# An RWKV recurrence whose triangular inverses are formed two groups at a time, in a loop pinned to its source order

## The chip, the cores and the metric

The kernel runs on one core of a Trainium2 chip. The metric is the device time of one execution in microseconds (us), from the runs shown below. TensorE (PE) does the matmuls, VectorE (DVE), ScalarE (ACT) and GpSimd (POOL) the elementwise work, and SyncE (SP) issues most DMA transfers. Each engine takes its instructions in the order in which the program lists them.

## What is computed

A trunk of two layers on 1024 tokens of 1024 channels in float32. Layer 0 mixes a gated convolution with differential attention, layer 1 is RWKV-7 time mixing; each is followed by a layer norm, a gated feed-forward network (FFN) and another norm. The change concerns the RWKV recurrence:

```
def wkv7_scan(r, w, k, v, a, b):                 # 16 heads x 64
    def step(S, inp):
        r_t, w_t, k_t, v_t, a_t, b_t = inp
        sa = jnp.einsum('bhvk,bhk->bhv', S, a_t)
        S = S * w_t[:, :, None, :] + sa[..., None] * b_t[:, :, None, :] + v_t[..., None] * k_t[:, :, None, :]
        return S, jnp.einsum('bhvk,bhk->bhv', S, r_t)
    ...

def rwkv7_time_mix(x, ...):
    ...
    o = wkv7_scan(r, decay, k, v, -kk, kk * a)
    mu = jnp.mean(o, -1, keepdims=True)
    var = jnp.mean(jnp.square(o - mu), -1, keepdims=True)
    o = ((o - mu) * lax.rsqrt(var + GN_EPS)) * gn_g + gn_b
    o = o + jnp.sum(r * k * r_k, -1, keepdims=True) * v
    return (o * g) @ w_o, v_first
```

## The kernel before

The program runs mixer 0 (to about 560 us), FFN 1 (to about 1200 us), the RWKV projections R, K and V with their preparation (to about 1655 us), the recurrence loop (to about 2011 us), and then the rest of the output projection and FFN 2.

The recurrence is computed in chunks of 64 tokens, in a form that replaces the token-by-token scan by matmuls and one triangular inverse for each chunk and head (formed in two blocks of 32 and joined). The work is cut into eight **units**: four quarters q of the tokens, two groups g of eight heads. The loop is `for i in range(n_u + 1)`. Each iteration calls `chunks` twice (h = 0 and 1), and each call works on two chunks at once, one of unit i-1 and one of unit i. The chain of one call is fixed by the data:

- S1 (PE, line 1410), copied to `xs` by ACT (1412); products `po` (1416) that wait for nothing else fill PE meanwhile;
- S2 (PE, 1421), copied to `xv` by ACT (1423);
- S3 (PE, 1430); DVE then forms `sm` (1432) and from it the next chunk's `xv` (1438, two for each chunk). S1 of the next call reads that `xv`;
- S4 (PE, 1444), the output, copied to `O` by ACT (1446).

Between these steps `chunks` calls `pump` four times, so p runs from 0 to 7 in an iteration: p0 and p4 lie between S1 and S2, p1 and p5 between S2 and S3, p2 and p6 between S3's DVE work and S4, p3 and p7 after S4. The table `PB` says which side work is issued at each pump, `PE_` which pieces of the output projection ("d") and loads for it ("e"). The side work:

- x, `prepare1` of unit i+3: four groups of matmuls `am` (1277) with a DVE multiply (1289), stores of `tD` and loads of `G`, then the inverse: for r = 1 to 30 a multiply (1310) and an add (1312) on DVE, and stores of the inverse in two layouts, `tT` and `tU` (1321, 1322). One unit has only 64 rows (two blocks of each of eight heads in four chunks), so `G` is loaded twice and the rows j of the inverse are split by parity over the two halves of the partitions.
- y, `prepare2` of unit i+1: loads of `TT` and `xs` from these stores (1354, 1356), two groups of small matmuls `mg` (1367, 1374), the copies `pm` on DVE (1369), and the loads of `xs`, `xv` and `rb` (1382 to 1386).
- z, `prepare3` of unit i+1: `am` products, a POOL multiply and the transposes `bt` (1339); g, the gates.
- t, `finish`, the **tail** of unit i-2, a group norm: on DVE a sum `gmu` (1453), a scale and a subtraction (1456); on ACT a square (1459); on DVE a sum (1461) and a scale (1462); on POOL a power (1463); on DVE a product (1464); then on PE the transposes `yt` (1472) in two groups of four. Its four steps are issued at p3, twice at p4, and at p5.

Products read operands from two tiles `bk` and `z` that are loaded anew for each group of eight matmuls (1268, 1271). In the V-projection stage ahead of the loop the table `VS` issues steps of the chain `pre`, which prepares the first units.

A scheduler sets each engine's order from dependences and priorities. S1 to S3 are marked with `high_priority`; otherwise an instruction may be put on its engine well before or after the place it has in the source. In FFN 1 a region is already under `manual_schedule(engines=ORDERED)`, where PE, DVE and ACT keep the order of the source; the recurrence loop is not.

Of the kernel before, what the change touches and what calls it, by code (L numbers as in the profile page):

```python
# [10 lines left out]
F32 = mybir.dt.float32  # L11
# [5 lines left out]
P = 128  # L17
# [24 lines left out]
PB = {"0": "y1 x1 g1 x1", "1": "g1", "2": "g0 y1 x1", "3": "g1 y1 t1 x1", "4": "x0 y1 x1 g1 t1 t1 g0", "5": "z1 g1 x0 g0 t1", "6": "z1", "7": "g1 x1 z1 g1"}  # L42
# [18 lines left out]
class Kern:  # L61
# [798 lines left out]
    def rwkv(self, xf, then):  # L860
# [419 lines left out]
        def prepare1(q, g, u):  # L1280

            XS = []
            tD = pd.tile([2, 32, 32, 32], F32, name=self.nm("tD"))
            for s in range(2):
                xs = self.U("xs")
                bk, zv = chunk_operands(q, g, s, 0)
                for i in range(2):
                    pv = chunk_products(bk, zv, i)
                    nc.vector.tensor_mul(xs[:, i * 512:i * 512 + 512].rearrange("p (h c t) -> p h c t", h=2, t=64), pv, mbc[0])
                    if i == 1:  # L1290
                        xv = xs.rearrange("p (h t) -> p h t", t=64)
                        for b in range(2):
                            nc.sync.dma_start(tD[b, s * 16:s * 16 + 16].rearrange("h s t -> s h t"), xv[s * 64 + b * 32:s * 64 + b * 32 + 32, :, b * 32:b * 32 + 32])
                    yield
                XS.append(xs)
            u["XS"] = XS
# [4 lines left out]
            yield  # L1301
            R = self.W("R", F32)
            Gv = G.rearrange("p (s t) -> p s t", t=32)
            Rv = R[:, :512].rearrange("p (j t) -> p j t", t=32)
            for pa in range(2):
                nc.vector.tensor_copy(Rv[half(pa)], G[half(pa), :].rearrange("p (j a t) -> p j a t", a=2, t=32)[:, :, pa, :])
            for r in range(1, 31):
                nj, nt = (r + 1) // 2, 31 - r
                tv = R[:, 512:512 + nj * nt].rearrange("p (j t) -> p j t", t=nt)
                nc.vector.tensor_tensor(tv, Rv[:, :nj, r:r + 1].broadcast_to([P, nj, nt]),  # L1310
                                        Gv[:, r:r + 1, r + 1:].broadcast_to([P, nj, nt]), op=ALU.mult)
                nc.vector.tensor_add(Rv[:, :nj, r + 1:], Rv[:, :nj, r + 1:], tv)
                if r in (8, 16):
                    yield
            for pa in range(2):
                nc.vector.memset(R[half(pa), :512][:, pa::34], 1.0)
            nc.vector.tensor_copy(G[:, :512].rearrange("p (t j) -> p t j", j=16), Rv.rearrange("p j t -> p t j"))
            tT = pd.tile([2, 32, 16, 2, 32], F32, name=self.nm("tT"))
            tU = pd.tile([32, 32, 32], F32, name=self.nm("tU"))
            for pa in range(2):  # L1320
                nc.sync.dma_start(tT[:, :, :, pa, :].rearrange("b h j t -> (b h) j t"), Rv[half(pa)])
                nc.sync.dma_start(tU[:, :, pa * 16:pa * 16 + 16], G[pa * 64:pa * 64 + 32, :512].rearrange("p (t j) -> p t j", j=16))
            u["tT"], u["tU"] = tT, tU
            yield
# [21 lines left out]
        def prepare2(q, g, u):  # L1346
# [4 lines left out]
            for s in range(2):  # L1351
                nc.gpsimd.memset(tv[64 * s + 32:64 * s + 64, :, 0:32], 0.0)
                for b in range(2):
                    nc.sync.dma_start(tv[64 * s + 32 * b:64 * s + 32 * b + 32, :, b * 32:b * 32 + 32],
                                      tT[b, s * 16:s * 16 + 16].rearrange("h j a t -> (j a) h t"))
                nc.sync.dma_start(XS[s].rearrange("p (h t) -> p h t", t=64)[s * 64:s * 64 + 32, :, 0:32],
                                  tU[s * 16:s * 16 + 16].rearrange("h t j -> t h j"))
# [10 lines left out]
            for s in range(2):  # L1368
                nc.vector.tensor_copy(pm[hi[s], :].rearrange("p (h j a) -> p h j a", a=2, j=16), pt[hi[s], :512].rearrange("p (h a j) -> p h j a", a=2, j=16))
# [119 lines left out]
        p1, p2, p3 = ((lambda i, f=f: f(*units[i], U_[i]) if i < n_u else none) for f in (prepare1, prepare2, prepare3))  # L1489
# [6 lines left out]
        pre = chain(p1(0), p1(1), p3(0), p2(0), p1(2))  # L1496
# [31 lines left out]
        tail = none  # L1528
        for i in range(n_u + 1):
            g1, g2, g3, tl = p1(i + 3), p2(i + 1), p3(i + 1), tail  # L1530
            count = [0]

            def pump():
                p = count[0]
                count[0] += 1
                for a in PB.get(f"{p}", "").split():
                    drain({"x": g1, "y": g2, "z": g3, "g": gen, "t": tl}[a[0]], int(a[1:]))
# [12 lines left out]
            drain(g1)  # L1550
            tail = finish(*units[i - 1], U_[i - 1]["O"]) if i else none
        for _ in range(5):
# [158 lines left out]
```

## Time and profile before

| | us |
|---|---|
| median of 3 runs | 2770.09 (2766.3 to 2771.7) |
| profiled execution | 2769.9 |
| its span, first to last instruction | 2768.1 |
| PE busy in the span | 2596.0 (94%) |
| DVE busy | 1937.0 (70%) |
| recurrence loop, first copy of S1 to the end of the last unit | 348, of which PE is busy 280.42 and DVE 253.80 |
| the loop's units, in order | 49, 37, 46, 46, 38, 39, 31, 38, 24 |

A unit here is the stretch from the first copy `xs` (line 1412) of one iteration to that of the next. The profile counts an engine as busy while it executes an instruction; PE's time includes matmuls that run at the lower of its two clock levels, 1.2 GHz. PEclk is the granted clock as a share of the full 2.4 GHz.

### The profile page before, as it was taken

How to read it: one execution, taken by the hardware profiler on the slowest of the kernel's cores; microseconds unless marked ns; L12 is line 12 of the kernel's file. 1: busy time of each engine (PE TensorE's matmuls, PEld its weight loads, DVE VectorE, ACT ScalarE, POOL GpSimd, SP SyncE). 2: the span in 40 equal slices, each digit the busy share in tenths (PEclk: the TensorE clock that was granted, in tenths of full speed). 3: DMA queues.
4: the chain of work that ended last, by engine and by line, in shares of the span. 5: the costliest groups of instructions: out<-in, count | busy, mean ns of one | idle time of the engine just before them, and what ended most of it. 6: DMA issues, size and time to landing. Idle time of an engine off the chain costs nothing. (4 is left out here: it accounts for less than half of the span.)

```text
span 2768.1 us, 37639 instructions
## 1 busy us (share of the span) xinstructions
PE 2596.0 (94%) x14736; PEld 2133.1 (77%) x14736; DVE 1937.0 (70%) x3013; ACT 1123.2 (41%) x1706; POOL 275.4 (10%) x247
## 2 busy tenths in 40 slices
PE   8999989989999999999997988688898999999998
PEld 6777778778888888877876766677776888888887
DVE  4655655598888865667778656786758888887673
ACT  3333332344444441426676223333425444444330
POOL 0000000100000003010011011343420000000000
PEclk9999999999999999999998999887999999999999
DMA  5111223212222273633256678786441222225660
GB/s 168 54 46 44 73 88 110 85 61 92 76 84 92 73 264 117 218 128 114 91 183 236 221 219 234 182 195 171 174 147 46 94 82 92 76 84 184 230 217 31
DMA packets 208674, 358.07 MB, mean 129 GB/s; under 512 B 88944, under 2 KB 118256, under 8 KB 208496
## 3 DMA queue, kind: packets, MB, share of 16 engines
q1 hardware_dynamic: 198704, 320.01, 36.5%
q0 software_dynamic: 9792, 35.66, 3.4%
q8 instruction: 116, 1.90, 0.3%
q14 instruction: 62, 0.51, 0.1%
HBM read 255.46 MB, written 95.94 MB: 127 GB/s over the span
## 5 line engine op out<-in xcount | busy, mean ns | idle before, releaser
L137 PE MATMUL up<-x,wu 128*128 128x512 f32 x1232 | 481.8, 393 | 18.5 <-DVE u L312 8.2
L138 PE MATMUL up<-x,wu 128*128 128x512 f32 x1232 | 482.9, 392 | 0.3 <-DVE x L145 0.2
L139 PE MATMUL up<-x,wu 128*128 128x512 f32 x1232 | 482.0, 391 | 0.0
L137 PEld LDWEIGHTS up<-x,wu 128*128 128x128 f32 x1232 | 232.8, 189 | 71.0 <-ACT x L144 14.4
L138 PE MATMUL dn<-wdl,gt 128*128 128x512 f32 x704 | 273.7, 389 | 0.0
L137 PE MATMUL dn<-wdh,gt 128*128 128x512 f32 x704 | 272.2, 389 | 0.3 <-ACT xf L179 0.3
L139 PE MATMUL dn<-wdh,gt 128*128 128x512 f32 x704 | 272.3, 389 | 0.0
L138 PEld LDWEIGHTS up<-x,wu 128*128 128x128 f32 x1232 | 233.1, 189 | 50.7 <-DVE x L145 2.7
L139 PEld LDWEIGHTS up<-x,wu 128*128 128x128 f32 x1232 | 233.0, 189 | 48.7
L254 ACT CAST wu<-ws 128x512 fp32r<-128x512 f32 x176 | 109.3, 623 | 288.4 <-PE up L139 198.8
L137 PE MATMUL pr<-xv,wph 128*128 128x512 f32 x384 | 154.0, 405 | 9.7 <-DVE kp L1156 7.7
L137 PE MATMUL pj<-x,wih 128*128 128x512 f32 x384 | 153.1, 409 | 7.5 <-ACT x L144 7.5
L115 DVE TENSOR_TENSOR wdl<-raw,wdh 128x1024 fp32r<-128x1024 f32 x88 | 109.7, 1246 | 68.7 <-ACT wdh L114 55.5
L138 PE MATMUL pr<-xv,wph 128*128 128x512 f32 x384 | 153.9, 401 | 3.5 <-DVE xv L915 3.5
L139 PE MATMUL pr<-xv,wpl 128*128 128x512 f32 x384 | 154.2, 402 | 2.6 <-DVE wpl L115 2.6
L139 PE MATMUL pj<-x,wil 128*128 128x512 f32 x384 | 153.8, 401 | 0.2 <-DVE wil L115 0.2
L138 PE MATMUL pj<-x,wih 128*128 128x512 f32 x384 | 153.8, 400 | 0.0
L137 PEld LDWEIGHTS dn<-wdh,gt 128*128 128x128 f32 x704 | 132.2, 188 | 27.8 <-ACT xf L179 0.5
L138 PEld LDWEIGHTS dn<-wdl,gt 128*128 128x128 f32 x704 | 132.2, 188 | 27.7 <-DVE wdl L115 0.3
L139 PEld LDWEIGHTS dn<-wdh,gt 128*128 128x128 f32 x704 | 132.2, 188 | 27.3
L114 ACT CAST wdh<-raw 128x1024 fp32r<-128x1024 f32 x88 | 92.6, 1052 | 108.6 <-DMA raw<-wdn 103.5
L254 ACT CAST wu<-wr 128x512 fp32r<-128x512 f32 x132 | 81.4, 623 | 125.1 <-PE up L139 62.8
(319 smaller groups left out, 5230.8 us busy)
## 6 DMA issues: line engine op xcount, KB each, us to landing
wr<-wup SPq DMA_DIRECT2D x88, 512.0 KB, 4.2
raw<-wdn SPq DMA_DIRECT2D x88, 512.0 KB, 4.2
G<-cv POOLq DMA_DIRECT2D x44, 512.0 KB, 2.9
gr<-G SPq DMA_DIRECT2D x88, 256.0 KB, 4.1
bk<-bkS SPq DMA_DIRECT2D x32, 512.0 KB, 5.9
res<-spill SPq DMA_DIRECT2D x24, 512.0 KB, 4.6
raw<-win SPq DMA_DIRECT2D x22, 512.0 KB, 3.7
spill<-res SPq DMA_DIRECT2D x16, 512.0 KB, 2.8
```

Source lines behind the costliest of these rows:

```text
L114: self.nc.scalar.copy(hi, raw)
L115: self.nc.vector.tensor_sub(lo, raw, hi.bitcast(F32))
L137: nc.tensor.matmul(ps, ah, bh, start=first, stop=False, **kw)
L138: nc.tensor.matmul(ps, ah, bl, start=False, stop=False, **kw)
L139: nc.tensor.matmul(ps, al, bh, start=False, stop=last, **kw)
L254: nc.scalar.copy(t[:, lo], src)
```

## The change

1. `prepare1` now treats both groups g of a quarter at once. The 128 partitions hold (g, block, head), so nothing is doubled: 30 multiplies and 30 adds now serve two units, each on r*(31-r) elements in a row (30 to 240) in place of ((r+1)//2)*(31-r). The two parity copies, and the permutation in the `pm` copies, go; the reordering copy of `G` moves from DVE to ACT; `R` is loaded by a DMA of its own; the stores of `tT` and `tU` become whole rows.
2. `prepare1` has 16 steps for each pair: eight products, the loads, six pieces of five r each, and a final one. A table `XB` says in which unit and pump each is issued. All of quarter 0 and 11 of the 16 steps of quarter 1 lie ahead of the loop. Quarter 1's rest is in unit 0; quarter 2 has its products in unit 0, its inverse at p5 to p7 of unit 1 and p0 to p2 of unit 2, and quarter 3 the same two units later.
3. The loop is put under `manual_schedule(engines=ORDERED)`: PE, DVE and ACT keep the order of the source. SP and POOL are still scheduled.

Lines of the new file are two higher up to `prepare1` and two lower from line 1354 on.

```
-PB = {"0": "y1 x1 g1 x1", "1": "g1", "2": "g0 y1 x1", "3": "g1 y1 t1 x1", "4": "x0 y1 x1 g1 t1 t1 g0", "5": "z1 g1 x0 g0 t1", "6": "z1", "7": "g1 x1 z1 g1"}
+PB = {"0": "y1 x g1", "1": "x g1", "2": "y1 x", "3": "g1 y1 t1 x", "4": "y1 x g1 t1 t1", "5": "z1 g1 x t1", "6": "x z1", "7": "g1 x z1 g1"}
+XB = {0: ("1 2", "1 2", "1 2", "1 2", "2", "1 2", "2", "2"), 1: ("2", "", "", "", "", "2", "2", "2"),
+      2: ("2 3", "2 3", "2 3", "3", "2 3", "3", "3", "3"), 3: ("3", "", "", "", "", "3", "3", "3"), 4: ("3", "3", "3", "", "3")}
...
-            G = self.U("G")
-            tDf = tD.rearrange("b h s t -> (b h) (s t)")
-            nc.sync.dma_start(G[0:64, :], tDf)
-            nc.sync.dma_start(G[64:128, :], tDf)
+            G, R, tmp = self.U("G"), self.U("R"), self.H("tv")
+            tDf = tD.rearrange("g b h s t -> (g b h) (s t)")
+            nc.sync.dma_start(G, tDf)
+            nc.sync.dma_start(R, tDf)
...
-            for pa in range(2):
-                nc.vector.tensor_copy(Rv[half(pa)], G[half(pa), :].rearrange("p (j a t) -> p j a t", a=2, t=32)[:, :, pa, :])
             for r in range(1, 31):
-                nj, nt = (r + 1) // 2, 31 - r
-                tv = R[:, 512:512 + nj * nt].rearrange("p (j t) -> p j t", t=nt)
-                nc.vector.tensor_tensor(tv, Rv[:, :nj, r:r + 1].broadcast_to([P, nj, nt]),
-                                        Gv[:, r:r + 1, r + 1:].broadcast_to([P, nj, nt]), op=ALU.mult)
-                nc.vector.tensor_add(Rv[:, :nj, r + 1:], Rv[:, :nj, r + 1:], tv)
-                if r in (8, 16):
+                nt = 31 - r
+                tv = tmp[:, :r * nt].rearrange("p (j t) -> p j t", t=nt)
+                nc.vector.tensor_tensor(tv, Rv[:, :r, r:r + 1].broadcast_to([P, r, nt]),
+                                        Gv[:, r:r + 1, r + 1:].broadcast_to([P, r, nt]), op=ALU.mult)
+                nc.vector.tensor_add(Rv[:, :r, r + 1:], Rv[:, :r, r + 1:], tv)
+                if r % 5 == 0:
                     yield
...
-            nc.vector.tensor_copy(G[:, :512].rearrange("p (t j) -> p t j", j=16), Rv.rearrange("p j t -> p t j"))
+            nc.scalar.copy(G.rearrange("p (t j) -> p t j", j=32), Rv.rearrange("p j t -> p t j"))
...
-            for pa in range(2):
-                nc.sync.dma_start(tT[:, :, :, pa, :].rearrange("b h j t -> (b h) j t"), Rv[half(pa)])
-                nc.sync.dma_start(tU[:, :, pa * 16:pa * 16 + 16], G[pa * 64:pa * 64 + 32, :512].rearrange("p (t j) -> p t j", j=16))
+            nc.sync.dma_start(tT.rearrange("g b h j t -> (g b h) (j t)"), R)
+            for g in range(2):
+                nc.sync.dma_start(tU[g].rearrange("h t j -> h (t j)"), G[g * 64:g * 64 + 32, :])
...
-        pre = chain(p1(0), p1(1), p3(0), p2(0), p1(2))
+        pre = chain(part(p1[0], 9), part(p1[1], 4), part(p1[0], 6), p3(0), p1[0], part(p1[1], 5), p2(0), part(p1[1], 2))
...
+        region = ExitStack()
+        region.enter_context(self.tc.manual_schedule(engines=ORDERED))
         for i in range(n_u + 1):
...
+                    if a == "x":
+                        for j in XB.get(i, ("",) * 8)[p:p + 1]:
+                            for c in j.split():
+                                drain(p1[int(c)], 1)
+                        continue
...
+        region.close()
```

The change moves instructions. Three places follow; a tile's name carries a running number.

PE, iteration 4 of the loop, before: the end of S3 (L1430) of call h = 0 and the start of S1 (L1410) of h = 1, with the tail's first transposes `yt` of unit 2 (L1472) and operands of `prepare3` (L1277, L1339) put among its matmuls.

```order
L1430 MATMUL sq_14568<-xv_14336,bkt_14481 64x64
L1410 MATMUL sq_14796<-xv_13828,xs_12651 64x64
L1416 MATMUL po_14797<-xv_13828,rb_13826 64x64
L1472 MATMUL yt_14857<-ident,O_13562 128x128 x4
L1277 MATMUL am_14890<-z_11379,bk_14886 128x128 x4
L1339 MATMUL bt_14897<-ident,bk_14886 128x128 x4
L1410 MATMUL sq_14796<-xv_13832,xs_12753 64x64
```

PE at the same place after: the end of the `po` products (L1414), then `yt` (now L1470), then S2 (L1419) for both chunks, the operands of `prepare3` (L1279, L1337), the second `yt`, and S3 (L1428).

```order
L1414 MATMUL po_14551<-xv_14140,rb_14138 64x64
L1414 MATMUL po_14551<-xv_14144,rb_14138 64x64
L1470 MATMUL yt_14615<-ident,O_13404 128x128 x4
L1419 MATMUL sq_14550<-xs_14560,TT_13443 64x64 x8
L1419 MATMUL sq_14550<-xs_14570,TT_13947 64x64 x8
L1279 MATMUL am_14648<-z_11379,bk_14644 128x128 x4
L1337 MATMUL bt_14655<-ident,bk_14644 128x128 x4
L1470 MATMUL yt_14661<-ident,O_13404 128x128 x4
L1428 MATMUL sq_14550<-xv_13700,bkt_13764 64x64
```

All four transposes of the first group now stand after S1 and its products and ahead of S2, and S2 and S3 stand behind them.

DVE, iteration 5, before: the tail of unit 3 (L1453, L1454, L1456) among the recurrence's `sm` and `xv` (L1432, L1438) of call h = 0 and an inverse (L1310, L1312).

```order
L1432 TENSOR_TENSOR sm_14918<-sq_14796,ST 128x256
L1310 TENSOR_TENSOR R_14965<-R_14965,G_14843 128x110
L1440 TENSOR_TENSOR ST<-sm_14918,gc 128x256
L1312 TENSOR_TENSOR R_14965<-R_14965 128x5x22
L1453 TENSOR_REDUCE gmu_15257<-O_14066 128x16
L1310 TENSOR_TENSOR R_14965<-R_14965,G_14843 128x105
L1454 TENSOR_SCALAR gmu_15257<-gmu_15257 128x16
L1312 TENSOR_TENSOR R_14965<-R_14965 128x5x21
L1456 TENSOR_TENSOR O_14066<-O_14066,gmu_15257 128x1024
L1432 TENSOR_TENSOR sm_14929<-sq_14796,ST 128x256
L1310 TENSOR_TENSOR R_14965<-R_14965,G_14843 128x120
L1438 TENSOR_TENSOR xv_14332<-sm_14929,gc 64x256
L1438 TENSOR_TENSOR xv_14336<-sm_14929,gc 64x256
```

DVE, iteration 5, after: `sm` and `xv` of call h = 0 (L1430, L1436), the `pm` copies (L1367), then the whole tail of unit 3 (L1451 to L1462).

```order
L1430 TENSOR_TENSOR sm_14849<-sq_14758,ST 128x256
L1436 TENSOR_TENSOR xv_14590<-sm_14849,gc 64x256
L1436 TENSOR_TENSOR xv_14594<-sm_14849,gc 64x256
L1367 COPY pm_14855<-mg_14854 32x512 x2
L1451 TENSOR_REDUCE gmu_14943<-O_13908 128x16
L1452 TENSOR_SCALAR gmu_14943<-gmu_14943 128x16
L1454 TENSOR_TENSOR O_13908<-O_13908,gmu_14943 128x1024
L1459 TENSOR_REDUCE gvr_14996<-Y_14994 128x16
L1460 TENSOR_SCALAR gvr_14996<-gvr_14996 128x16
L1462 TENSOR_TENSOR O_13908<-O_13908,gvr_14996 128x1024
```

The tail's first sum moved from between the two `sm` to behind both chunks' `xv` and the `pm` copies; the inverse is not in this iteration any more.

SP at the loop's start, before: the loads of unit 0's operands `xv` and `rb`, the last store of `vS` but one, and the stores of products `tD`; unit 0's loads of `TT` stand 20 rows further up.

```order
L1384 DMA xv_12425<-vS_8475 64x4x256
L1386 DMA rb_12423<-rS_8479 64x4x256
L1384 DMA xv_12429<-vS_8475 64x4x256
L1244 DMA vS_8476<-vtok_12402 128x8x128
L1386 DMA rb_12423<-rS_8479 64x4x256
L1250 DMA bvS_8474<-bv_12223 128x1024
L1271 DMA z_11379<-aS_8478 64x2x256 x2
L1293 DMA tD_12432<-xs_12433 32x16x32 x2
```

SP at the loop's start, after: the last `vS` store, a `z`, the joint loads of `G` and `R`, unit 0's `TT` (L1352) and then its `xs`, `xv` and `rb` (L1380 to L1384).

```order
L1246 DMA vS_8476<-vtok_12392 128x8x128
L1273 DMA z_11380<-aS_8477 64x2x256
L1302 DMA G_12413<-tD_11787 128x1024
L1303 DMA R_12414<-tD_11787 128x1024
L1252 DMA bvS_8474<-bv_12273 128x1024
L1352 DMA TT_12418<-tT_12298 32x16x32 x4
L1380 DMA xs_11447<-aS_8477 64x4x256
L1382 DMA xv_12500<-vS_8475 64x4x256
L1384 DMA rb_12498<-rS_8479 64x4x256
L1380 DMA xs_11539<-aS_8477 64x4x256
L1382 DMA xv_12504<-vS_8475 64x4x256
```

Unit 0's loads of `TT`, `xs`, `xv` and `rb` moved from ahead of the last `vS` stores to behind the loads of `G` and `R` for quarter 1.

## Rows read from the trace of the kernel before

**Rows 1.** Windows of the loop: length; busy PE, PEld, DVE, ACT, POOL; clock; DMA; GB/s.

```profile
1749.00:1795.00 46.00, 33.81 (x564) 30.45 (x566) 40.23 (x112) 16.65 (x37) 22.10 (x19) 0.87 0.72 177
...
1841.00:1879.00 38.00, 28.79 (x520) 25.45 (x516) 35.97 (x87) 15.25 (x34) 18.27 (x15) 0.89 0.76 186
...
sum 348.00, PE 280.42 PEld 239.51 DVE 253.80 ACT 124.04 POOL 130.22; mean PE 31.16 PEld 26.61 DVE 28.20 ACT 13.78 POOL 14.47
```

**Rows 2.** Groups of DVE instructions in the loop, shapes apart: count, busy, mean ns, idle.

```profile
L1438 DVE TENSOR_TENSOR xv<-sm,gc 64x256 f32<-64x256 f32 x48 | 26.9, 561 | 0.9
...
L1432 DVE TENSOR_TENSOR sm<-sq,ST 128x256 f32<-128x256 f32 x30 | 12.6, 419 | 28.5 <-PE sq L1430 28.5
...
L1369 DVE COPY pm<-mg 32x512 f32<-32x512 f32 x14 | 9.7, 690 | 5.6 <-PE mg L1367 5.4
...
L1310 DVE TENSOR_TENSOR R<-R,G 128x30 f32<-128x30 f32 x12 | 2.2, 187 | 0.2
...
L1310 DVE TENSOR_TENSOR R<-R,G 128x128 f32<-128x128 f32 x6 | 1.7, 290 | 0.2
```

**Rows 3.** Waits of PE in the loop: us in total, times, longest.

```profile
PE sq L1410 <- DVE xv L1438: 24.6, 6, 8.4
...
PE am L1277 <- issue: 12.3, 4, 5.6
...
PE am L1277 <- DMA bk<-bkS: 11.4, 4, 6.0
...
PE yt L1472 <- DVE O L1464: 2.2, 1, 2.2
```

**Rows 4.** Windows, two neighbouring stretches of units 4 to 6.

```profile
1877.40:1894.50 17.10, 16.53 (x290) 14.60 (x288) 14.16 (x43) 3.74 (x10) 3.75 (x2) 0.50 0.72 171
1894.50:1911.60 17.10, 13.94 (x216) 12.18 (x214) 6.76 (x16) 9.91 (x23) 11.64 (x10) 1.00 0.48 99
```

**Rows 5.** Timeline of PE, S1 in these stretches: start us, us, then idle before.

```profile
1877.20 0.33 PE L1410 MATMUL sq<-xv,xs 128*64 128x64 f32 x2 [4.98 <-DVE xv L1438]
...
1878.10 1.11 PE L1410 MATMUL sq<-xv,xs 128*64 128x64 f32 x14
...
1895.29 0.68 PE L1410 MATMUL sq<-xv,xs 128*64 128x64 f32 x14
```

**Rows 6.** Timeline, the tail of unit 7, alone after the loop.

```profile
2011.83 1.22 DVE L1453 TENSOR_REDUCE gmu<-O 128x16 f32<-128x1024 f32 x1 [1.00 <-ACT O L1446]
...
2013.30 1.22 DVE L1456 TENSOR_TENSOR O<-O,gmu 128x1024 f32<-128x1024 f32 x1
...
2014.69 1.06 ACT L1459 ACTIVATE Y<-O 128x1024 f32<-128x1024 f32 x1 [2.89 <-DVE O L1456]
...
2016.30 1.21 DVE L1461 TENSOR_REDUCE gvr<-Y 128x16 f32<-128x1024 f32 x1
...
2018.28 2.92 POOL L1463 TENSOR_TENSOR gvr<-gvr,mhalf 128x16 f32<-128x16 f32 x1 [8.93 <-DVE gvr L1462]
...
2021.74 1.22 DVE L1464 TENSOR_TENSOR O<-O,gvr 128x1024 f32<-128x1024 f32 x1
```

**Rows 7.** Timeline of SP and PE at the loop's start.

```profile
1620.17 2.22 SPq L1354 DMA_DIRECT2D TT<-tT  x4
...
1662.12 1.07 SPq L1293 DMA_DIRECT2D tD<-xs  x2
...
1644.02 0.39 PE L137 MATMUL pr<-xv,wph 128*128 128x512 f32 x1
...
1644.24 0.39 PE L138 MATMUL pr<-xv,wph 128*128 128x512 f32 x1
...
1660.70 0.33 PE L1410 MATMUL sq<-xv,xs 128*64 128x64 f32 x2
```

**Rows 8.** DMA issues from 1500 to 2012 us: count, KB, median us to landing.

```profile
tD<-xs SPq DMA_DIRECT2D x32, 64.0 KB, 3.7
...
xv<-vS SPq DMA_DIRECT2D x16, 256.0 KB, 6.5
```

More of the change, by code (lines that the diff above doesn't have):

```diff
@@ new lines, in prepare1 @@
+        def prepare1(q, us):
+            tD = pd.tile([2, 2, 32, 32, 32], F32, name=self.nm("tD"))
+            for g in range(2):
+                us[g]["XS"] = XS = []
+                for s in range(2):
+                    xs = self.U("xs")
+                    XS.append(xs)
+                    bk, zv = chunk_operands(q, g, s, 0)
+                    for i in range(2):
+                        pv = chunk_products(bk, zv, i)
+                        nc.vector.tensor_mul(xs[:, i * 512:i * 512 + 512].rearrange("p (h c t) -> p h c t", h=2, t=64), pv, mbc[0])
+                        if i == 1:
+                            xv = xs.rearrange("p (h t) -> p h t", t=64)
+                            for b in range(2):
+                                nc.sync.dma_start(tD[g, b, s * 16:s * 16 + 16].rearrange("h s t -> s h t"), xv[s * 64 + b * 32:s * 64 + b * 32 + 32, :, b * 32:b * 32 + 32])
+                        yield
+            G, R, tmp = self.U("G"), self.U("R"), self.H("tv")
+            tDf = tD.rearrange("g b h s t -> (g b h) (s t)")
+            nc.sync.dma_start(G, tDf)
+            nc.sync.dma_start(R, tDf)
+            yield
+            Gv, Rv = (x.rearrange("p (s t) -> p s t", t=32) for x in (G, R))
+            for r in range(1, 31):
+                nt = 31 - r
[4 more added lines that the diff above has]
+                if r % 5 == 0:
+                    yield
+            nc.vector.memset(R[:, ::33], 1.0)
+            nc.scalar.copy(G.rearrange("p (t j) -> p t j", j=32), Rv.rearrange("p j t -> p t j"))
+            tT = pd.tile([2, 2, 32, 32, 32], F32, name=self.nm("tT"))
+            tU = pd.tile([2, 32, 32, 32], F32, name=self.nm("tU"))
+            nc.sync.dma_start(tT.rearrange("g b h j t -> (g b h) (j t)"), R)
+            for g in range(2):
+                nc.sync.dma_start(tU[g].rearrange("h t j -> h (t j)"), G[g * 64:g * 64 + 32, :])
+                us[g]["tT"], us[g]["tU"] = tT[g], tU[g]
@@ L1368, in prepare2 @@
             for s in range(2):
[L1369 removed]
+                nc.vector.tensor_copy(pm[hi[s], :], pt[hi[s], :])
             yield
@@ L1488, in rwkv @@
         none = iter(())
-        p1, p2, p3 = ((lambda i, f=f: f(*units[i], U_[i]) if i < n_u else none) for f in (prepare1, prepare2, prepare3))
+        p2, p3 = ((lambda i, f=f: f(*units[i], U_[i]) if i < n_u else none) for f in (prepare2, prepare3))
+        p1 = [prepare1(q, U_[2 * q:2 * q + 2]) for q in range(4)]
         def chain(*gens):
```

34 lines of the change are left out of this document (4 added, 30 removed).

## Prediction

> **What bounds the kernel now.** I read the page first, for shares: PE is busy 94% of the span, so a change can gain only in stretches where PE waits. The recurrence loop is the largest: PE is busy 280.42 of 348 us there, and 67.6 us are open [rows 1]. Next I read the windows by unit: in the units of 46 and 38 us shown, DVE is busy 40.23 and 35.97 us while PE has 33.81 and 28.79 us of work [rows 1]. There DVE sets the pace. The waits of PE say how: S1 waits for `xv` from DVE 24.6 us in six waits, and the products `am` wait 12.3 and 11.4 us for issue and for `bk` [rows 3]. In the order of before, one sees in the unit shown that `sm` and `xv` stand behind pieces of the tail and of an inverse on DVE. So the loop is bound by the recurrence, held up by side work ahead of it on DVE and by reloads. The clock adds to it: after a wait of 4.98 us before S1 [rows 5] the granted clock was 0.50 for 17.1 us, then 1.00 [rows 4], that is the 1.2 and the 2.4 GHz level; 14 matmuls of S1 took 1.11 us at the one and 0.68 us at the other [rows 5].
>
> **Joint inverse.** From 187 ns at 30 elements and 290 ns at 128 [rows 2], an instruction costs 157 ns plus 1.05 ns for each element, as an estimate. A unit before has 30 multiplies and 30 adds on 2600 elements each: 60 x 0.157 + 2 x 2600 x 0.00105 = 14.9 us, 29.8 us for a pair. A joint inverse has 60 instructions for both, on 4960 elements: 9.4 + 10.4 = 19.8 us. So DVE is spared 10 us in a pair, and some copies. In the loop before did six inverses (units 2 to 7), 89 us; after does two joint ones and four of six pieces of quarter 1, some 54 us. DVE has 35 us less, of 253.80. The largest new shape (240 elements) is in no row; by the line it takes 0.41 us, by the row at 128 not under 0.29 us, and since about 70 instructions in the loop have over 200 elements, an error of 0.1 us is 7 us on an engine that will no longer set the pace. I count it at nothing.
>
> **What this gives on the path.** The six waits for `xv`, 24.6 us [rows 3], should mostly go, by the smaller inverse and because the pinned order puts both `xv` ahead of the tail. A piece of five r costs 2.4 to 4.0 us (10 x 0.157 plus 820 to 2320 elements). At p2 and p6 a piece lies behind `xv` and beside S4; at p1 and p5 it stands right ahead of the next `sm`, at p0, p4 and p7 a little earlier. I let each joint inverse delay S1 by 4 us; with the parts in the loop (2.7 of them) and the slack of p0, about 9 us stay. Term: -16 us (ends -24.6 and -5). The `am` waits, 23.7 us [rows 3], stand at products and at `prepare3`. Units 1, 3 and 4 have no products any more, and in each iteration from 2 on PE will reach `prepare3` late, for the reason in the next part, while its loads run on. Two reloads in units 0 and 2 stay. Term: -20 us (ends -24 and -8).
>
> **The pinned tail.** This is the cost. Alone after the loop the tail takes from 2011.83 to 2021.74 + 1.22, that is 11.1 us, the handovers between DVE, ACT and POOL included, the power on POOL 2.92 of it [rows 6]. Before, the scheduler started it as soon as `O` was complete, so that PE waited for it once, 2.2 us [rows 3]. After, DVE comes to its first sum only behind both chunks' `sm` and `xv` and the two `pm` copies, which from the end of S3 is 2 x 0.42 + 4 x 0.56 (up to 0.59) + 2 x 0.69 = 4.5 us [rows 2]. So the first `yt` can run 4.5 + 11.1 = 15.6 us after S3 of call h = 0. PE has up to there: `pm`'s second products (they wait those 4.5 us, then about 0.7 us), S1 with its 32 matmuls and 32 `po`: by 0.68 us for 14 [rows 5] about 3 us, where the operand is there; some 8 us, and in the first units one or two gate products more, 10 to 12 us. PE then stands 3.6 to 7.6 us at `yt`, and S2 and S3 are queued behind it, as the order shows: the recurrence itself waits. I take 5.5 us for each of the seven iterations that have a tail (2 to 8), 38.5 us, less the 2.2 us of before. Term: +36 us (ends: 2 and 8 us each, +12 and +54). DVE, ACT and the DMA queues are not behind that wait, which is why I credit the reloads above.
>
> **The clock.** Before, six waits of S1 were long enough to bring stretches like that at 0.50 [rows 4]; after, seven waits at `yt` take their place. I count this at nothing. The Trainium skill, in "TensorE: Matmul & The Clock Gate", section "HAM oscillation — how this bites in real kernels", says that where PE waits between bursts, each burst starts at the lower clock. The trace agrees at the one place shown, and the rule speaks against this change, since every tail gets such a wait; it is part of the third rival.
>
> **The loop's start.** Unit 0's S1 began at 1660.70 us; `TT` had been asked for at 1620.17 us [rows 7]. After, the loads of `TT`, `xs`, `xv` and `rb` stand on SP behind the joint `G` and `R`, which wait until the products' stores have landed, 3.7 us after their issue [rows 8]. Those stores were issued at 1662.12 us before, for the products of another unit [rows 7]. If they come at that time, `G` goes at about 1666, four `TT` take 2.22 us [rows 7], and `xv` lands 6.5 us after its issue [rows 8]: S1 at about 1676, 15 us late. If the products are done early, in the V-projection, where PE has work to put between, nothing is late. I take +13 us, nearer to the row (ends 0 and +17). What PE does meanwhile, gates and products, it has not to do later; the 13 us are what I leave after that.
>
> **Output projection.** By the order 18 matmuls fewer of it stand inside the loop. They follow behind it, where PE has no gaps; neighbouring matmuls of that width start 0.22 us apart [rows 7], so +4 us (ends 0 and +4).
>
> **At nothing.** The copies by parity are gone from DVE, the reordering copy of `G` on ACT lies beside PE (ACT is busy 124.04 of 348 us [rows 1]). The stores of `tT` and `tU` in whole rows take less of the DMA engines; that is in the `am` term.
>
> **Sum.** -16 - 20 + 36 + 13 + 4 = +17 us against the profiled execution of 2769.9 us, which is 0.2 us under the median of 2770.09: 2787 us.
>
> **Rivals.**
>
> *Faster.* The relief counts whole, and the tail is hidden. For: DVE is busy 87 to 95% in the two units shown [rows 1], and every wait of S1 is for DVE [rows 3]. If the tail's own instructions take their bare 1.22 + 1.22 + 1.06 + 1.21 + 2.92 + 1.22 us and little between, and gates keep PE busy to about 12 us, 2 us a unit are left: +12. With -24 and -17, +7 at the start and +4: -18, so 2752 us. Against: gates are spent in the later units, and the tail was measured alone, so its handovers are real.
>
> *No change.* The loop's relief -26, tails +12, start +10, projection +4: 0, so 2770 us. It needs the start as forecast, and the tail at its low end.
>
> *Much slower.* Each tail wait is 5.5 us and is followed by a stretch at the lower clock, in which the three chain steps of two chunks, six groups of 16, lose some 0.43 us each [rows 5]: 2.6 us a tail, 18 us. With -26 of relief, +36, +13 and +4: +45, so 2815 us. It decides if the stretches of before [rows 4] do not shrink with the waits for `xv`.
>
> *The change does not do what it says*: the joint inverse is not cheaper, say by 0.1 us more for each large instruction. That is 7 us of DVE over two to three units, beside work of PE; its chance is within that of the forecast.
>
> **How the numbers follow.** Forecast 0.42 (2776 to 2800 us), much slower 0.13, faster 0.33, no change 0.12. About 0.2% or 5.5 us is what a measurement of this kernel can tell from no change, so 2764.6 to 2775.6 us is "same". Slower: 0.42 + 0.13 = 0.55; same 0.12; faster 0.33. Faster spreads about 2752 by some 12 us, since the start and the `am` term vary by that much; a third of it lies under 2746. Half of the slowest case lies over 2812. That leaves out 0.11 and 0.07: range 2746 to 2812 us.
>
> **What would show it.** In the changed profile's waits of PE, `yt` behind the tail's product on DVE should be the first entry, near 38 us in seven waits; S1 behind `xv` should have fallen under 12 us. If `yt` has under 15 us, the tail term is wrong, and the kernel is faster. The first S1 should come near 1675 us; if it comes by 1665, the start term is wrong. DVE's busy time in the loop should be near 219 us. If the loop is about 348 us long but PE's clock in it is lower than before, the clock term was not nothing.

## The result and the profile after

The changed kernel takes 2858.81 us (2857.12 to 2862.18, 4 runs) against 2768.81 us before: 1.0333 times as long, interval 1.0314 to 1.0353. The forecast was 2787 us, with a range up to 2812 us. The sign was right, the size was not: +90 us against +17.

The span grew from 2768.1 to 2857.6 us. The first copy of S1 came at 1685.1 us (1663.4 before), 21.7 us later; from there to the last copy of `O` it took 408.3 us (348.0), 60.3 us more; and from there to the end 764.2 us (756.6), 7.6 us more.

Windows of the kernel after, four of the loop's units (1, 2, 4 and 5), then the first eight together, then the loop to the last copy of `O`; columns as in [rows 1].

```profile
1737.00:1770.00 33.00, 26.39 (x504) 23.35 (x504) 14.64 (x30) 13.07 (x31) 9.18 (x10) 0.84 0.70 188
1770.00:1828.00 58.00, 35.27 (x568) 31.73 (x568) 34.61 (x72) 17.01 (x35) 17.92 (x15) 0.82 0.51 130
1869.00:1923.00 54.00, 29.57 (x504) 26.50 (x504) 34.75 (x67) 16.39 (x33) 18.71 (x17) 0.62 0.43 116
1923.00:1964.00 41.00, 29.60 (x504) 26.48 (x504) 13.83 (x19) 15.21 (x35) 17.75 (x15) 0.67 0.49 122
...
1685.00:2059.00 374.00, 251.90 (x3918) 221.77 (x3918) 190.72 (x324) 120.51 (x248) 121.54 (x100) 0.74 0.53 149
...
1685.00:2093.40 408.40, 275.59 (x4101) 240.21 (x4100) 205.61 (x344) 128.94 (x262) 126.36 (x104) 0.75 0.52 147
```

The same eight units of the kernel before:

```profile
1663.00:1987.00 324.00, 256.57 (x3964) 220.31 (x3960) 234.96 (x566) 116.24 (x248) 122.30 (x100) 0.84 0.75 195
```

The reader is to see three things. VectorE is busy 190.72 us in place of 234.96, so the joint inverse did what it says. PE has about as much to do (3918 matmuls in the rows, 3964 before), but of 374 us it has 251.90 busy, so 122 us are open where there were 67; over the whole loop it is busy 275.59 us, 280.42 before [rows 1], so what the loop gained in length is waiting. And the unit without a tail and without a long wait behind pieces (unit 1) takes 33 us; one with a tail (unit 5) 41; those with a tail and with pieces ahead of `sm` (2 and 4) 58 and 54.

PE's waits in the loop after, which answer to [rows 3]: us in total, times, longest.

```profile
PE yt L1470 <- DVE O L1462: 43.1, 6, 8.6
PE sq L1428 <- DVE sm L1430: 29.3, 13, 12.6
PE sq L1419 <- ACT xv L1421: 12.4, 14, 1.3
PE sq L1408 <- ACT xs L1410: 11.2, 13, 1.3
PE am L1279 <- DMA z<-aS: 7.9, 2, 6.7
PE yt L1470 <- DVE tv L1309: 5.5, 1, 5.5
PE sq L1428 <- ACT xv L1421: 5.5, 6, 0.9
```

`yt`, 2.2 us in [rows 3], is now 48.6 us in seven waits: its first row, and the one whose last releaser was a piece of the inverse (L1309). S1's wait for `xv`, 24.6 us in [rows 3], is gone; S3's wait for `sm`, 2.2 us before, is 29.3 us. New are 29.1 us in which PE stands for a copy of ScalarE (S2 for `xv`, S1 for `xs`, S3 for `xv`) 33 times, each about a microsecond; before, the chain's waits for such copies were 2.2 us.

One tail, in unit 5 of the kernel after. Timeline of VectorE: start us, us, then the idle time before.

```profile
1934.47 1.22 DVE L1451 TENSOR_REDUCE gmu<-O 128x16 f32<-128x1024 f32 x1
...
1941.07 1.22 DVE L1459 TENSOR_REDUCE gvr<-Y 128x16 f32<-128x1024 f32 x1 [3.92 <-ACT Y L1457]
...
1945.55 1.23 DVE L1462 TENSOR_TENSOR O<-O,gvr 128x1024 f32<-128x1024 f32 x1 [3.05 <-POOL gvr L1461]
```

Timeline of ScalarE, the square:

```profile
1939.99 1.06 ACT L1457 ACTIVATE Y<-O 128x1024 f32<-128x1024 f32 x1
```

Timeline of GpSimd, the power:

```profile
1942.58 2.94 POOL L1461 TENSOR_TENSOR gvr<-gvr,mhalf 128x16 f32<-128x16 f32 x1 [10.04 <-DVE gvr L1460]
```

Timeline of PE, `po`, `yt` and S2:

```profile
1939.42 1.97 PE L1414 MATMUL po<-xv,rb 64*64 64x64 f32 x32
1946.92 1.08 PE L1470 MATMUL yt<-ident,O 128*128 128x128 f32 x4 [5.53 <-DVE O L1462]
1947.94 1.12 PE L1419 MATMUL sq<-xs,TT 64*64 64x64 f32 x16
```

The sum `gmu` starts at 1934.47, behind `xv` and `pm`; the product ends at 1946.78, 12.3 us later. The square waits on ScalarE behind `xs`, the copy that follows S1. PE is through with `po` at 1941.39, waits 5.53 us, does the transposes and only then S2, whose operands were there before.

### The profile page after: what moved, and what is told of

Same layout as the page of the kernel before. It is cut to its first block, busy times and chain, and to the rows that moved or that the text cites. A ratio compares the mean times of both kernels' runs of the same rounds, so it can differ in the third digit from the quotient of the medians.

```text
span 2857.6 us, 37279 instructions
## 1 busy us (share of the span) xinstructions
PE 2595.6 (91%) x14736; PEld 2137.9 (75%) x14736; DVE 1891.6 (66%) x2737; ACT 1132.7 (40%) x1710; POOL 274.9 (10%) x247
```

## Experiments

Each is one kernel against the kernel before on the same chip; "the change" is the changed kernel.

### Which part costs: joint inverse or pin

The joint inverse without the pin:

```
-        region = ExitStack()
-        region.enter_context(self.tc.manual_schedule(engines=ORDERED))
...
-        region.close()
```

> The joint inverse, its steps placed as in the change, with the loop left to the scheduler. Theory 1, the pinned order costs the time (tail ahead of S2, handovers in the open): this kernel keeps the gain on VectorE and loses none of it there, so 2755 to 2785 us, with the first S1 still some 10 to 20 us late, and PE's wait for yt under 5 us. Theory 2, the joint inverse in itself is the loss (long pieces ahead of sm, loads late): it is still slower by over 40 us, 2810 us or more, with S3 waiting for sm by over 15 us.

Measured: 2774.45 us, ratio 1.0026 (1.0014 to 1.0037). The kernel before with the pin and nothing else:

```
+        region = ExitStack()
+        region.enter_context(self.tc.manual_schedule(engines=ORDERED))
         for i in range(n_u + 1):
...
+        region.close()
```

> The kernel before with nothing but its loop pinned to the source order. Theory 1: the tail waits (48.6 us in the change) and the handovers to ScalarE and VectorE (29 us) come with the order alone, and VectorE has 60 instructions of inverse for each unit in one or two blocks besides, so 2850 us or more. Theory 2: the order alone costs little, under 30 us, so below 2800 us.

Measured: 2877.08 us, ratio 1.0389 (1.0366 to 1.0411). Its first waits of PE in the loop:

```profile
PE sq L1430 <- DVE sm L1432: 59.7, 13, 14.7
PE yt L1472 <- DVE O L1464: 47.8, 7, 9.4
```

So theory 1 holds in the main: both times lie in its ranges, and without the pin PE hardly waits for `yt`. One sign of theory 2 is there too: without the pin S3 waits 19.3 us for `sm`, 12.1 us of it at once, and the first S1 is 24.6 us late, more than the 10 to 20 expected. The pin costs 110 us on the old inverse and 84 us on the joint one; the joint inverse costs 7 us without the pin and saves 18 us with it (2877 to 2859; some 15 us by the two ratios), where S3's wait for `sm` falls from 59.7 to 29.3 us.

### Which engine's order

```
-        region.enter_context(self.tc.manual_schedule(engines=ORDERED))
+        region.enter_context(self.tc.manual_schedule(engines={mybir.EngineType.PE}))
```

> The change with only PE held to the source order in the loop; VectorE and ScalarE are left to the scheduler. Theory 1, PE's order is what costs (yt ahead of S2, each second group behind the copy of the first): most of the 84 us between the change and the unpinned joint inverse stays, 2835 us or more, with yt waits of 30 us or more. Theory 2, VectorE's order costs (tail and pieces ahead of sm): with it free the time is under 2800 us.

Measured: 2815.38 us, ratio 1.0174 (1.0151 to 1.0197). And the other two engines, `engines=ORDERED - {mybir.EngineType.PE}`:

> The change with VectorE and ScalarE held to the source order and PE free. Theory 1 (PE's order costs): PE fills its waits with other work as in the kernel before, so under 2800 us and yt waits under 10 us. Theory 2 (VectorE's and ScalarE's order costs): the tail comes late all the same and the recurrence waits for sm behind pieces, 2835 us or more.

Measured: 2839.38 us, ratio 1.0261 (1.0241 to 1.0281). Waits of PE in the loop, with PE held:

```profile
PE sq L1428 <- DVE sm L1430: 22.4, 13, 10.4
PE sq L1408 <- ACT xs L1410: 16.6, 12, 3.6
PE sq L1419 <- ACT xv L1421: 14.1, 14, 1.7
```

The same with VectorE and ScalarE held:

```profile
PE yt L1470 <- DVE O L1462: 46.4, 6, 10.2
PE sq L1428 <- DVE sm L1430: 16.1, 6, 12.4
...
PE yt L1470 <- DVE tv L1309: 5.8, 1, 5.8
...
PE sq L1408 <- ACT xs L1410: 5.0, 4, 1.2
```

Neither theory holds whole. PE's order alone costs 41 us (against 2774), and with it PE waits for `yt` 3.8 us in all: the scheduler starts the tail early on VectorE, and the place of `yt` on PE does no harm. What PE's order costs are the handovers to ScalarE (42 us in all its waits for `xs` and `xv`); S3's wait for `sm`, 22.4 us, is near the 19.3 us that it is without any pin. The order of VectorE and ScalarE costs 65 us, and brings the wait for `yt` (52.2 us) although PE's order is free. The two together cost 84 us, less than their sum. So the late tail on VectorE and ScalarE is the cause of the wait at `yt`. Which of these two engines' orders it is no run separates; in the trace above VectorE's first sum comes late, and the square then waits 2.8 us more behind `xs`.

### The tail earlier

The change with the steps of the tail at p0, p1, p2, p4 and p5 (its square is issued with the first step, and the product is a step of its own):

```
-PB = {"0": "y1 x g1", "1": "x g1", "2": "y1 x", "3": "g1 y1 t1 x", "4": "y1 x g1 t1 t1",
+PB = {"0": "t1 y1 x g1", "1": "t1 x g1", "2": "y1 t1 x", "3": "g1 y1 x", "4": "y1 x g1 t1",
```

> The change with the tail's elementwise steps issued earlier in the iteration: sum, subtraction and square at p0, second sum and power at p1, product at p2, transposes at p4 and p5 as in the change. Theory 1: PE's waits for yt (48.6 us in seven waits) go to under 8 us, and the time falls by 35 to 50 us, to 2809 to 2824 us. Rival: the wait only moves, since sm of call h = 0 now stands behind the second sum, or the clock keeps the stretch; then the time falls by under 20 us, to over 2839 us.

Measured: 2819.78 us, ratio 1.0183 (1.0165 to 1.0202), 39 us less than the change: theory 1. The waits for `yt` are down to 1.5 us. Part of the wait moved, as PE's waits in the loop show:

```profile
PE sq L1419 <- ACT xv L1421: 29.6, 14, 12.4
PE sq L1428 <- DVE sm L1430: 22.7, 13, 4.8
```

S2's wait for ScalarE rose from 12.4 to 29.6 us, since the square, which waits for VectorE, now stands ahead of the copies `xv` on ScalarE. The longest, 12.4 us, is in unit 4: there the tail's subtraction stands behind the pieces on VectorE, and so it is the change's wait for `sm` in another place.

### The handovers

S1, S2 and S3 issue the matmuls of both chunks ahead of the copies or sums that read the first; of S1 for example:

```
+                for q, g, u, c, ps, po in at:
                     xs = self.S(256, "xs")
                     nc.scalar.copy(xs, ps[:, 0:256])
```

> The change with S1, S2 and S3 of both chunks issued on PE ahead of the copies and sums that read them. In the change PE waits for the copy of the first chunk before it starts the second chunk's group: 11.2 us at S1, 12.4 at S2, some 8 at S3 beside the two long ones. Theory: these go, the time falls by 10 to 30 us, to 2829 to 2849 us. Rival: the first chunk's copy starts 0.7 us later at each step and PE waits the same time one step on, so no gain over 5 us.

Measured: 2840.12 us, ratio 1.0256 (1.0233 to 1.0279), 19 us less than the change, as the theory said. PE's waits for ScalarE's copies in the chain fell from 29.1 to 10.4 us. S3's waits for `sm` did not go away with them: PE now meets the same delay one step on, at `mg` behind the `pm` copies, 31.9 us in twelve waits. In the change the second chunk's group waited for the first chunk's copy although it reads nothing of it: both write one PSUM tile (`sq`), and the program waits at that matmul for ScalarE. The scheduler of before had put other matmuls there.

### The pieces, and the start

Quarter 2's and 3's pieces are issued at other pumps:

```
-XB = {0: ("1 2", "1 2", "1 2", "1 2", "2", "1 2", "2", "2"), 1: ("2", "", "", "", "", "2", "2", "2"),
-      2: ("2 3", "2 3", "2 3", "3", "2 3", "3", "3", "3"), 3: ("3", "", "", "", "", "3", "3", "3"), 4: ("3", "3", "3", "", "3")}
+XB = {0: ("1 2", "1 2", "1 2", "1 2", "2", "1 2", "2", "2"), 1: ("2", "", "2", "2", "", "", "2", "2"),
+      2: ("3", "3", "2 3", "2 3", "2 3", "3", "3", "3"), 3: ("3", "", "3", "3", "", "", "3", "3"), 4: ("", "", "3", "3", "3")}
```

> The change with only the places of the inverse's six pieces moved: to p2, p3, p6, p7 of one unit and p2, p3 of the next, behind both chunks' xv and never at p0, p1 or p5 ahead of sm. In the change S3 waits for sm 8.3 us in unit 2 and 12.6 us in unit 4 behind a run of such pieces. Theory: these two waits go, units 2 and 4 (58 and 55 us) come near units 3 and 5 (41 us), and the time falls by 15 to 25 us, to 2834 to 2844 us. Rival: the pieces now stand ahead of the tail or of sm of the next call, the wait comes back at yt or at S3, and the time falls by under 8 us.

Measured: 2855.46 us, ratio 1.0317 (1.0298 to 1.0335), 3 us less, which the intervals don't tell from the change. The rival holds; the waits changed places, as PE's waits from the loop's start on show:

```profile
PE yt L1470 <- DVE O L1462: 61.7, 7, 13.0
PE sq L1428 <- DVE sm L1430: 15.4, 13, 5.1
```

S3's waits for `sm` halved, from 29.3 to 15.4 us, and those for `yt` rose by 13 us, since the pieces at p2 and p3 now stand ahead of the tail's first sum and among its steps. In the change the block at the start of unit 4 looked like this on VectorE (timeline):

```profile
1864.79 2.37 DVE L1309 TENSOR_TENSOR tv<-R,G 128x150 f32<-128x150 f32 x1
1867.20 1.27 DVE L1311 TENSOR_TENSOR R<-R,tv 128x150 f32<-128x150 f32 x1
...
1886.94 0.42 DVE L1430 TENSOR_TENSOR sm<-sq,ST 128x256 f32<-128x256 f32 x1
1887.39 1.18 DVE L1436 TENSOR_TENSOR xv<-sm,gc 64x256 f32<-64x256 f32 x2
```

and on PE:

```profile
1872.15 0.68 PE L1419 MATMUL sq<-xs,TT 64*64 64x64 f32 x16 [0.86 <-ACT xv L1421]
1873.74 1.07 PE L1428 MATMUL sq<-xv,bkt 128*64 128x64 f32 x16 [0.91 <-ACT xv L1421]
1887.41 1.12 PE L1428 MATMUL sq<-xv,bkt 128*64 128x64 f32 x16 [12.59 <-DVE sm L1430]
```

From 1864.79 to 1886.94 VectorE does nothing but the inverse (r = 6 to 25, the four pieces of p6, p7, p0 and p1), `sm` stands behind it, and PE waits 12.59 us with the second chunk's S3.

The loads of unit 0 ahead of the last steps of quarter 1:

```
-        pre = chain(part(p1[0], 9), part(p1[1], 4), part(p1[0], 6), p3(0), p1[0], part(p1[1], 5), p2(0), part(p1[1], 2))
+        pre = chain(part(p1[0], 9), part(p1[1], 4), part(p1[0], 6), p3(0), p1[0], p2(0), part(p1[1], 7))
```

> The change with the loads of unit 0's operands issued in the V-projection ahead of the last products of quarter 1, in place of behind them. Theory: unit 0's first copy of S1, at 1685 us in the change and 1663 us before, comes to 1662 to 1670 us, and the time falls by 12 to 22 us, to 2837 to 2847 us. Rival: the products and the inverse of quarter 1 that now come later are missed at once, in units 0 and 1, and less than half of the gain is left.

Measured: 2862.11 us, ratio 1.0349 (1.0325 to 1.0374), nothing gained. The first S1 came 14 us earlier, at 1671.1 us, but unit 0 took 71.2 us in place of 52.1. PE waits there 12.3 us once for a product's multiply behind the inverse of quarter 1. So the place of the loads is not what the late start costs: the last products and the inverse of quarter 1 were done during it, and unit 0 now waits for them.

### All four moves

> The pinned change with four moves at once: the tail's steps early, S1 to S3 of both chunks ahead of their copies, the pieces at p2, p3, p6 and p7, and unit 0's operands early. If the four costs lie one behind the other, their gains add: 39 us and 19 us as measured, some 20 and 17 us as expected of the other two, so about 2764 us. If they lie beside each other, as waits of the same chain, the sum is not reached: 2780 us or more.

Measured: 2798.85 us, ratio 1.0117 (1.0099 to 1.0135), 60 us less than the change. It is over 2780 us, as the second expectation has it, but the gains do add: measured alone they were 39, 19, 3 and -3 us, which makes 58. The expectation's sum took 20 and 17 us for the last two. From the first copy of S1 in unit 1 to that after unit 7 this kernel takes 257.2 us, the kernel before 275.1. Unit 0 takes 75 us; PE stands there behind pieces, since a product's multiply (L1294) is queued behind them, as one row of its timeline shows:

```profile
1698.38 2.08 PE L1279 MATMUL am<-z,bk 128*128 128x128 f32 x8 [13.59 <-DVE xs L1294]
```

The largest of this kernel's waits of PE is another:

```profile
PE sq L1430 <- ACT xv L1423: 30.3, 9, 14.2
```

On ScalarE `xv` stands behind the tail's square, and where the wait is longest, in unit 4, the square waits for a subtraction that stands behind a block of pieces on VectorE. So the block costs PE a wait of 12 to 17 us in unit 4 of four pinned kernels, at a different place in most: at `sm` in the change (12.6), at `xv` with the tail early (12.4) and here (14.2), at `pm` with S1 to S3 grouped (17.0). No run has the pieces out of the way of all of them.

The same kernel with the preparation earlier (three more slots in the V-projection's table, eight steps in all, where the expectation says six: `"3m": "q2", "3e": "q2"` and `"5e": "q2 q2"`) and in each pump products ahead of pieces:

```
+XB = {0: ("2 1", "2 1", "2 1", "2 1", "2", "2 1", "2", "2"), 1: ("2", "", "2", "2", "", "", "2", ""),
+      2: ("3", "3", "3 2", "3 2", "3", "3", "3 2", "3 2"), 3: ("3", "", "3", "3", "", "", "3", ""), 4: ("", "", "3", "3", "", "", "3", "3")}
```

> The pinned change with all four moves, the preparation six steps earlier, and in each pump the products of quarter 2 ahead of the pieces of the inverse before, none of them right ahead of a tail. With the four moves alone unit 0 takes 75 us (48 us in the kernel before) since PE waits 13.6 us for a product's multiply behind pieces and 10 us for operands. Theory: unit 0 falls to 50 to 60 us, the time to 2775 to 2785 us. Rival: unit 0 stays over 70 us, and the time over 2790 us.

Measured: 2792.85 us, ratio 1.0096 (1.0076 to 1.0116). Unit 0 stayed long, at 77.3 us, and the time is over 2790 us: the rival. What would shorten unit 0 stays open.

### Where the gain of the joint inverse goes without the pin

The unpinned joint inverse takes 1688.0 to 2014.2 us from the first copy of S1 to the last of `O`, 21.8 us less than before, but starts 24.6 us later. So the start was moved here too, by the same line as above.

> The joint inverse with the loop left to the scheduler (2774 us) and unit 0's operands issued ahead of the last products of quarter 1. Theory: the loop of that kernel from the first to the ninth copy of S1 is 294.7 us, 28.5 us shorter than before, and it only starts 24.6 us late; with the start at 1662 to 1672 us the time falls by 13 to 25 us, to 2749 to 2761 us, under the kernel before. Rival: the loop was short because work was done during the late start, so the gain is under 8 us and it stays at 2766 us or more.

Measured: 2767.82 us, ratio 1.0007 (0.9994 to 1.0020), the time of the kernel before. In its profiled execution the start is 9.0 us later than before and the loop 19.5 us shorter; that execution had a span of 2759.5 us, under the median of its runs, so the runs don't bear out the whole of it. In unit 3 (50.3 us) the scheduler, too, puts a block of the inverse ahead of `sm`. Timeline of VectorE in that kernel, two `sm` in a row:

```profile
1813.86 0.42 DVE L1430 TENSOR_TENSOR sm<-sq,ST 128x256 f32<-128x256 f32 x1
...
1841.33 0.39 DVE L1430 TENSOR_TENSOR sm<-sq,ST 128x256 f32<-128x256 f32 x1
```

and of PE, the end of S4's `po` and the second chunk's S3:

```profile
1829.43 0.57 PE L1442 MATMUL po<-xv,ar 128*64 128x64 f32 x13
1841.77 1.12 PE L1428 MATMUL sq<-xv,bkt 128*64 128x64 f32 x16 [11.76 <-DVE sm L1430]
```

Between the two `sm` lie 27 us, and PE waits 11.76 us. The block is not all of it: six instructions of the inverse between these `sm` took 1.3 to 2.8 us in place of some 0.4, 9.5 us more together, and each ran beside an elementwise operation of GpSimd (see the last section). The longest, in the timeline of VectorE:

```profile
1828.72 2.75 DVE L1311 TENSOR_TENSOR R<-R,tv 128x238 f32<-128x238 f32 x1
```

It ends at 1831.47; beside it GpSimd issues a DMA transfer until 1829.20 and is in a multiply (line 1334) from 1829.22 to 1830.50. So without the pin there are two candidates for this wait, the place of the block and its length, and the runs don't separate them. Three more kernels followed: the preparation earlier (`VS` as above),

> The unpinned joint inverse with unit 0's operands early (2768 us) and the preparation spread over more places of the V-projection, six steps earlier. Theory: the first copy of S1 comes to about 1663 us and quarter 1's inverse no longer fills units 0 to 2, so the loop keeps the 294.7 us of the kernel whose start was late: 2740 to 2755 us. Rival: the steps are put where the scheduler wants them anyway, and the time stays within 5 us of 2768 us.

measured 2772.49 us, ratio 1.0021 (1.0009 to 1.0034): the rival, no gain. The pieces apart,

> The unpinned joint inverse with unit 0's operands early (2768 us), its pieces issued at p2, p3, p6 and p7 in place of p0 to p2 and p5 to p7. In that kernel's trace one inverse runs in a block on VectorE in unit 3, the next sm stands behind it, PE waits 11.8 us and the unit takes 50 us. Theory: with the pieces issued apart, the scheduler puts sm between them, S3's waits for sm fall from 21.5 us to under 12 us and the time to 2750 to 2760 us. Rival: the scheduler gathers the pieces again wherever the source puts them, and the time stays within 5 us of 2768 us.

measured 2769.49 us, ratio 1.0022 (1.0010 to 1.0034): the rival again. S3's waits for `sm` are 19.5 us, the longest 14.1, and in unit 3 again 27 us lie between the same two `sm`: here the scheduler gathered the pieces although the source puts them apart. Six instructions of that block, too, took 1.3 to 2.8 us. And the two moves that helped under the pin,

> The unpinned joint inverse with unit 0's operands early, and the two moves that helped the pinned loop: the tail's steps early and S1 to S3 of both chunks ahead of their copies. Theory: these moves repair only what the pin broke; the scheduler already starts the tail when its data is there, so the time stays within 8 us of 2768 us. Rival: the source order guides the scheduler too, and the time falls to under 2757 us.

measured 2762.12 us, ratio 0.9991 (0.9978 to 1.0004): not told from the kernel before, and within the theory's 8 us of 2768. This fits two moves that only repair what the pin broke; no kernel here was clearly faster than the kernel before.

## Why the prediction was right or wrong

**The tail: right, somewhat small.** Forecast +36 us, waits of 5.5 us in seven iterations. The profile has 48.6 us in seven, 7 us each, +46 against before. In unit 5, where nothing else is near, the product ended 15.7 us after S3 (forecast 15.6), PE was there after 10.3 us, and the wait is 5.53 us, as forecast. The longer ones, up to 8.6 us, are in units 2, 4, 6, 7 and the last one, where VectorE has pieces or work of the output projection besides; the term had no price for that. Taking the waits away gave 39 us. The mechanism was as forecast: VectorE comes late to the first sum, and PE stands at `yt` ahead of S2. The runs with some engines held show that the first half decides: with VectorE and ScalarE held the wait is 52.2 us, with PE alone 3.8. That unit 5's wait is just the forecast's is in part luck: PE needed 10.3 us to get there, not some 8, by matmuls at the lower clock and a wait for `xs`.

**The handovers: missing.** This is the step that failed most: I gave the pinned order no cost but the tail. The 26.9 us of new waits for ScalarE are in no term. The order of after showed S1 and S2 of the two chunks back to back with nothing between, and the copies between them stood in the quoted function; the waits of before, 2.2 us, were the price with fills, not without. Grouping gave 19 us back.

**The `xv` term: wrong sign.** Forecast -16 us. S1's waits of 24.6 us went, and S3's waits for `sm` rose by 27.1: +2.5 in all. I priced the pieces one at a time and let a joint inverse delay S1 by 4 us. But p6, p7, p0 and p1 all lie between two successive `sm`, so four pieces run in one block: by my own line 40 x 0.157 + 2 x 4140 x 0.00105 = 15.0 us. The block took 22.1 us; five of its instructions took some 1 to 2 us longer than elsewhere at their size, 5.9 us together (see the last section). It cost 12.6 us of waiting in unit 4, the like of it 8.3 in unit 2. (By [rows 2] the line's constant is 156 ns, not 157, which changes no sum.)

**The `am` term: too large.** Forecast -20 us, from 23.7 to some 4. With a wait for `z` that the term left out (2.1 us) before had 25.8; the profile after has 16.8 us, -9. The waits for `bk` went, waits for `z` of 13.3 us came.

**The start: the chain right, its price and cause not.** Forecast +13 us, with S1 at about 1676, 15 us late; its first two matmuls came at 1679.5, the others at 1683.93, the copy at 1685.1, +21.7. The chain was as told. Timeline of SP after:

```profile
1666.88 0.49 SPq L1302 DMA_DIRECT2D G<-tD  x1
...
1668.41 3.91 SPq L1352 DMA_DIRECT2D TT<-tT  x4
...
1674.88 0.62 SPq L1382 DMA_DIRECT2D xv<-vS  x1
```

and of PE:

```profile
1664.96 1.20 PE L1365 MATMUL mg<-xs 32*32 32x32 f32 x64
1675.71 0.28 PE L1372 MATMUL mg<-TT,pm 32*32 32x32 f32 x2 [9.55 <-DMA TT<-tT]
...
1683.93 1.09 PE L1408 MATMUL sq<-xv,xs 128*64 128x64 f32 x14 [3.74 <-DMA xv<-vS]
```

`G` went at 1666.88 (forecast 1666); the four `TT` took 3.91 us in place of 2.22, and S1 waited for `xv`. But the run that starts 14 us earlier is no faster: what the start costs is the work for quarter 1 that is done there, and not the place of the loads.

**Output projection: about right.** 108 matmuls of it had started by the last copy of `O`, 128 before; forecast 18 fewer and +4 us, measured +7.6 behind the loop. Some 4 us of these are longer waits of PE there, 2.1 of them for `yhh` and `yhl`, the high and low part of the projection's operand.

**The clock: lower, but its cost is not shown.** Over the first eight units the granted clock is 0.74, before 0.84, the sign that the prediction had named, though for a loop no longer than before. Units 1 and 5 of the kernel after have 504 matmuls each: 26.39 us busy at a granted 0.84, 29.60 at 0.67. But against the kernel before PE's busy time in the loop did not rise (275.59 us, 280.42 before, with 69 matmuls fewer in the rows), so the rise of the loop stands in the waits; what the lower clock adds on the path the runs don't tell. The rival "much slower" had 18 us for it. The reason for counting it at nothing was weak all the same: of the six waits of S1 before, only four were over 3 us (8.4, 6.3, 5.0 and 3.1), and after has, beside the seven at `yt`, two long ones for `sm` (12.6 and 8.3). The Trainium skill, "TensorE: Matmul & The Clock Gate", section "HAM oscillation — how this bites in real kernels", has each burst behind such a wait start at the lower clock; these rows agree in direction.

**Sum by what the rows show.** Tail +46.4, handovers +26.9, `xv` and `sm` +2.5, `am` -9, start +21.7, behind the loop +7.6: +96 us, against 89.5 of the span. What these terms leave out goes both ways: some 8 us of small waits of before went, PE was busy 4.8 us less, and waits of the output projection in the loop rose by 6.5. The forecast was +17; it was short by 27 us at the handovers, 18.5 at `xv` and `sm`, 11 at `am`, 10 at the tail, 9 at the start and 4 behind the loop. The step that failed is the one that says which waits the order brings: I followed one instruction (`yt`) through the new order, put the handovers at nothing without a reason, and priced the pieces ahead of `sm` one at a time.

**The instruction count: right.** VectorE does 44 us less in the eight units and 48 in the whole loop (forecast 35, and some copies), and the largest shape took what the line gave, 0.41 us, as its group on VectorE (count, busy, mean ns, idle) shows beside that at 150 elements:

```profile
L1309 DVE TENSOR_TENSOR tv<-R,G 128x240 f32<-128x240 f32 x6 | 2.4, 406 | 0.2
...
L1309 DVE TENSOR_TENSOR tv<-R,G 128x150 f32<-128x150 f32 x6 | 4.0, 659 | 0.2
```

## What to carry to other kernels

When a scheduled loop is pinned to its source order, every place where the source puts a copy between two groups that could follow each other can become a wait, as it did 33 times here: go through one iteration on each engine, not through the instruction that moved most. Issue a tail as soon as its data is there and its readers late, and issue independent groups ahead of the copies that read them; these two moves gave 39 and 19 us here. A block of side work that several chains wait behind is not cured by moving the chains: four kernels here met it, at three places. Work taken off an engine is worth what its waits on the critical engine are worth, and these may come back elsewhere, as here at the start and ahead of `sm`.

## What the runs showed of the hardware

Instructions of the inverse that ran beside an elementwise operation of GpSimd took longer and ended just behind it. In the block of unit 4 the one at 1864.79 took 2.37 us and the next 1.27, where the same two took 0.32 and 0.32 us at 1676.44 and 1676.79, while GpSimd did nothing; the mean of that shape is 659 ns in the row above. GpSimd's timeline at that place:

```profile
1864.44 2.54 POOL L1479 TENSOR_TENSOR Y<-Y,gt 128x1024 f32<-128x1024 f32 x1
1866.95 1.34 POOL L1334 TENSOR_TENSOR ar<-ar,msk 128x512 f32<-128x512 f32 x1
```

The first ends at 1866.98, the second at 1868.29; the two instructions of VectorE end at 1867.16 and 1868.47, each 0.18 us later. The Trainium skill, "SBUF — State Buffer", section "Who interferes with whom", states that a DVE instruction with two SBUF inputs contends with a GpSimd instruction that reads SBUF; these rows agree. By the prediction's line the two would have taken 0.63 us together. Of the five long instructions in that block four end 0.2 us behind an elementwise operation of GpSimd, and the fifth ran beside GpSimd's issues of DMA transfers. In the unpinned kernel with the early start six such instructions make 9.5 us between two `sm`, where PE waits 11.76 us. No run here took GpSimd's work away, so what it costs in all was not measured.
